# A streaming encoder layer on one core: squares one step earlier, and the first turn of p ahead of the last product

## The chip, the core and the metric

The kernel runs on one core of a Trainium2 chip. The metric is the time of one execution on the device in microseconds (us). TensorE (PE) multiplies, VectorE (DVE), ScalarE (ACT) and GpSimd (POOL) work on tiles, and SyncE (SP), ACT and POOL issue transfers (DMA).

## What is computed

The reference is one layer of an encoder, over a prompt of 2048 frames and over 32 new frames of a running stream, and a last norm. Cut to what matters:

```python
hn = rmsnorm(h, g_mix)
hA, bA, cA, zA, vB, zB = split(hn @ w_in)            # 1024 -> 6 x 512
u = cA * hA;  c = conv3(u) + conv_b;  yA = bA * c * silu(zA)
pooled = trailing_means(vB, windows 2, 4, 8, 16) - vB
yB = (pooled @ pool_w) * pool_scale * silu(zB)
h = h + concat(yA, yB) @ w_out                        # 1024 -> 1024
gate = sigmoid(rmsnorm(h, g_ple) @ w_ple_gate)        # 1024 -> 1024
h = h + (p @ w_ple) * gate                            # the embedding: 256 -> 1024
y = rmsnorm(h, g_final)
```

The last rows of u and v are returned as states.

## The kernel before

All products are made in parts: each f32 operand is split into a high part (a cast, on ACT) and the rest (a subtraction, on DVE; `split`, L77), and a product is the sum of three matmuls of such parts. Most products of four quarters are formed with seven in place of eight, from sums of quarters, so DVE also adds and subtracts quarters of weights and of frames.

**First stage: w_in.** The 2080 frames are five blocks of 416, in three groups: blocks 0 and 1, blocks 2 and 3, block 4 (`GROUPS`, L27; the loop at L1134). Each group runs four units, one for each 128 channels. A unit of the first two groups makes three pairs of products (`Unit.seven`, L899): zb with v (names zbv), c with h (ch), za with b (zab). A pair (L859) has seven products of twelve matmuls into three banks X, Y, Z: X takes quarters 11, S2, S3 and 22, and between them its partial sums are read out. The product S3 can only start when ACT has copied the sum after S2 out (`carry`, L871), and the last product, 22, when DVE has added the sum after S3 into its place (`out`, L874; for zab this is the addition U<-x_zab).

While the second group computes, its spare time on the other engines prepares block 4 (`last_block`, L1059): it is handed to the pairs as `aside`, and for every three steps of the pairs one of its steps is taken (`at_pace`, L1164), from the second unit on. Block 4 has four pieces of rows (128, 128, 128, 32). For a piece c, `scale(c)` takes the squares of its rows with their sum (`x_stat`, L397, and `sumsq`, L87: one activation on ACT over 1024 columns, then two small instructions on POOL for the inverse root, L70 and L74), loads the next piece's rows, and scales the rows in four instructions on DVE (L1098, tile xs) that are kept in program order; POOL stores them (L1100), SP loads them back in blocks (xb, L1106), DVE turns them in place (L1112), and ACT and DVE split them in halves that POOL stores (b_d). In one step of `last_block` the squares, the root and the scaling of a piece come one directly after the other.

**Second stage: W_out.** Pairs of tiles of 128 frames run through `seven` (L211): X, Y, Z again, with calls that hang between the products (`between`). Called with `late`, it makes the products in this order: 11, S2, S1, S3 (all but the S1 add to X, which ends in the last), 12 with 21 (Y), S4 (Z), `step(6)` at L261, and 22 with T4 (X, the last; x_o<-wo_T, 12 matmuls). The loop is at L1288; its last pair is i = 14 (`NT - 3`). The short tile of 32 frames is made ahead of that pair.

**Third stage: the embedding.** `embed` (L105) makes p @ w_ple for the remaining 14 tiles. For a tile, `prep` loads p for four tiles at a time (ep, L122), turns it on PE with two transposes into a bank of its own (ptp, L131; there are two such banks), and splits it (pps, L132 by way of L78 and L79); `run` calls it up to two tiles ahead, makes two halves of six matmuls (e, L103), and ACT copies them out (L148) for a store. Its weight is loaded and split by `embedding_chunks` (wqr, wq, L1310). The embedding's first `prep` runs after the loop of W_out. Beside it ACT and DVE make the quarters of the gate weight (wg) from rows that SP loads (wg_r, L1343).

**Fourth stage: the gate.** Pairs of tiles again (x_g, y_g, z_g), the sum with h by accumulating transfers on POOL (L1396), and the last norm. Rows of h come back in blocks (hn, L1367) and are turned on DVE.

The order of the instructions on each engine is set by the scheduler that builds the program, from the order in which the code is written; instructions under `keep_in_program_order` keep their written order.

Of the kernel before, what the change touches and what calls it, by code (L numbers as in the profile page):

```python
# [9 lines left out]
F32 = mybir.dt.float32  # L10
F32R = mybir.dt.float32r
# [4 lines left out]
P = 128  # L16
D = 1024
# [9 lines left out]
NT = SEQ // P + 1  # L27
NH = D // 2
KH = KC // 2
EARLY = 3  # L30
LATE = 2
# [4 lines left out]
def trunk(ctx, tc, x_p, x_s, c_conv, c_pool, p_p, p_s, g_mix, w_in, conv_w, conv_b, pool_w,  # L36
# [16 lines left out]
    def bank(name):  # L53
        return ps_m.tile([P, 512], F32, tag="mm", name=name)
# [156 lines left out]
    def seven(name, A, W, carry, out, between={}, late=False, in_parts=False, first_tile=False):  # L211

        step = lambda c: between[c]() if c in between else None
        frames_late, weights_late = (FINE, FINE[::2] + FINE[1:2]) if in_parts else (None, None)  # L220
        X, Y, Z = (bank(f"{c}_{name}") for c in "xyz")

        def lower(*parts):
            for ks in parts:
                product(Z, A["S1"], W["T1"], P, ks.start == 0, ks)
            return carry(Z, (1, 1)) if ks.stop == KH else None

        parts = range(KH // 2), range(KH // 2, KH)
        product(X, A["11"], W["11"], P, True, order=frames_late)
        c1 = carry(X, (0, 0))  # L230
        step(1)

        def upper():
            product(Y, A["12"], W["21"], P, True, order=weights_late)
            out(Y, c1, (0, 0))

        if not late:
            upper()
        if in_parts:
            lower(parts[0])  # L240
        step(2)
        product(X, A["S2"], W["T2"], P, False)
        c2 = carry(X, (0, 1))
        step(3)
        c3 = lower(parts[1]) if in_parts else lower(range(KH))
        step(4)

        def right():
            product(Z, A["S4"], W["22"], P, False, order=weights_late)
            out(Z, c2, (0, 1))  # L250

        if first_tile:
            right()
        product(X, A["S3"], W["T3"], P, False)
        out(X, c3, (1, 1))
        step(5)
        if late:
            upper()
        if not first_tile:
            right()  # L260
        step(6)  # L261
        product(X, A["22"], W["T4"], P, False)
        out(X, None, (1, 0))
# [44 lines left out]
    def ring4(t, name):  # L308
        return t.tile([P, D], F32, tag="t", name=name)
# [21 lines left out]
    with ExitStack() as s1:  # L331
# [65 lines left out]
        def x_stat(x, later=False):  # L397

            t, n, name = x
            return t, n, sumsq(t, n, name, later=later)  # L400
# [79 lines left out]
        def staged(name):  # L480
            return xin.tile([P, KH, 2, P], F32R, tag="t", name=name)
# [107 lines left out]
        for c, x in enumerate([*ahead0, short0]):  # L589
            normal(x)  # L590
            n = P if c < 3 else DEC
# [442 lines left out]
        ahead = {}  # L1034

        def load_ahead(g, c):
            ahead[g, c] = columns_in(g, c) if g == 1 else [x_load(f"4_{c}", [x_rows(4, c)])]
# [21 lines left out]
        def last_block():  # L1059

            load_ahead(2, 0)
            back = {}

            def scale(c):
                x = x_stat(ahead.pop((2, c))[0], True)
                if c < 3:
                    load_ahead(2, c + 1)
                scaled_to_memory(x, c * P)
                return x[1]

            def halves_to_memory(c, n):
                u = turned_in_place(back.pop(c))
                for half in range(2):
                    t = staged(f"b_4_{c}_{half}")[:, :, :, :n]
                    v = lambda h: t[:, :, h].rearrange("p k (g t) -> p k g t", t=32)
                    tc.keep_in_program_order(split(v(0), v(1), u[:, half * KH:half * KH + KH]))
                    nc.gpsimd.dma_start(b_d[:, half * KH:half * KH + KH, :, c * P:c * P + n], t.bitcast(F32))
                    yield

            for c in range(5):  # L1080
                n = scale(c) if c < 4 else 0
                yield
                if c:
                    yield from halves_to_memory(c - 1, m)
                if n:
                    back[c], m = from_memory(c * P, n), n
                yield

        xs_d = tc.dram_tile([NB, D], F32, name="xs_d")
# [12 lines left out]
        def from_memory(r, n):  # L1102

            t = ring4(xin, f"xb_{r}")[:, :n * KC]
            for q in range(4):
                nc.sync.dma_start(t[q * 32:q * 32 + 32].rearrange("p (g c) -> p g c", c=256),  # L1106
                                  xs_d[r:r + n, q * 256:q * 256 + 256].rearrange("(g p) c -> p g c", p=32))
            return t
# [24 lines left out]
        for gi, tbs in enumerate(GROUPS):  # L1133
            if gi == 2:  # L1134

                frames_in.close()
                t = slot("hn_4")
# [3 lines left out]
                W = sums_slots("wo")  # L1141
                nc.sync.dma_start(g_bc, g_fin.partition_broadcast(P))
                ya = ctx.enter_context(tc.tile_pool(name="ya", bufs=5, side="right"))
# [31 lines left out]
    with ExitStack() as s2:  # L1175
        pool = lambda name, bufs: s2.enter_context(tc.tile_pool(name=name, bufs=bufs, reuse_waits="tile"))
        w3, qa, xh, st, ss, cmb = (pool(*a) for a in (
            ("w3", 1), ("qa", 1), ("xh", 3), ("st", 4), ("ss", 3), ("cmb", 8)))
# [13 lines left out]
        def h_ops(x, n, name, bare=False, two=False):  # L1192

            add = lambda o, a, b: nc.vector.tensor_tensor(o, a, b, op=ALU.add)

            def carry(ps, at):
                t = st.tile([P, NH], F32, tag="t", name=f"c_{name}_{at[0]}{at[1]}")
                if bare and at != (1, 0):
                    nc.scalar.copy(t[:n], ps[:n])  # L1199
                    return t  # L1200
                add(t[:n], ps[:n], half_of(x, at, n))
                if two:
                    add(t[:n], ps[n:2 * n], t[:n])
                return t

            def out(ps, c, at):
                t = half_of(x, at, n)
                if bare and at != (1, 0):
                    add(t, t, c[:n])
                    c = None  # L1210
                add(t, ps[:n], t if c is None else c[:n])
                if two:
                    add(t, ps[n:2 * n], t)

            return carry, out
# [61 lines left out]
        S = {}  # L1277
# [4 lines left out]
        def next_gate():  # L1282
# [2 lines left out]
                rest_gate()  # L1285
            waiting[:] = [scale_gate(k) for k in [next(gate_rows, None)] if k is not None]

        for i in range(0, NT - 1, 2):  # L1288
            with tc.issue_after(loaded[-1].ins):
                x = [load_rows(xh, "x", i + b, x_p) for b in range(2)] if i else [first_x, second_x]  # L1290
            seven(f"o{i}", S.pop(i), W, *h_ops(x, P, f"o{i}", i == 0), {0: {1: rest}, 2: {3: next_gate}}.get(i, {}), True, i == 0)
            for b in range(2):
                done_h(i + b, x[b])
            last = i + 4 == NT - 1
            if last:
                n = tiles[NT - 1][1]
                A = short("yl", load_y(NT - 1, n), n)
            if i + 2 < NT - 1:

                with tc.issue_after(loaded[-1].ins), tc.issue_after(hold[-1].ins):  # L1300
                    more = prep_h(i + 2)
                more()
            if last:
                x = load_rows(xh, "x", NT - 1, x_p, x_s)
                plain("ol", A, W, n, *h_ops([x], n, "ol", two=True))
                done_h(NT - 1, x)
            next_gate()


        def embedding_chunks(name, rings=(ya, ya)):  # L1310
            wp = []
            for k in range(2):
                raw = ring4(rings[k], f"{name}r_{k}")
                nc.sync.dma_start(raw, w_ple[k * P:(k + 1) * P])
                t = [cmb.tile([P, KH, 2, P], F32R, tag="c", name=f"{name}_{k}_{h}").rearrange("p a b c -> p (a b c)")
                     for h in range(2)]
                split(t[0], t[1], raw)
                wp.append(t)
            return wp

        wp = embedding_chunks("wq")

        rest_e = [*range(EARLY, NT - 2), NT - 1]

        def ring(what, i):
            if what == "pps":
                return st.tile([P, 2, 2, P], F32R, tag="t", name=f"pps_{i}")
            if what == "out" and i not in rest_e[-LATE:]:
                return cmb.tile([P, D], F32, tag="c", name=f"eout_{i}")
            return ring4(ya, f"e{what}_{i}")  # L1330

        _, run = embed(rest_e, wp, ring)
        for c in range(len(rest_e) - LATE):
            run(c)

# [1 line left out]
        W = sums_slots("wg")  # L1337
# [267 lines left out]
        S = {}  # L1605
        n = tiles[NT - 1][1]
# [5 lines left out]
        h, e = (load_rows(*a) for a in ((xh, "h", NT - 1, h_d), (ya, "e", NT - 1, e_d)))  # L1612
# [20 lines left out]
        for i in range(0, NT - 3, 2):  # L1633
            A = S.pop(i)
            steps = prep_g(i + 2)
            e = [load_rows(ya, "e", i + b, e_d) for b in range(2)]
# [32 lines left out]
```

## Time and profile before

| | |
|---|---|
| time, median of 3 runs | 920.71 us (919.93 to 922.12) |
| the profiled execution's own time | 921.88 us |
| its span | 920.1 us |
| PE busy | 906.1 us, 98% of the span |
| weight loads (PEld) busy | 820.7 us, 89% |
| DVE busy | 722.8 us, 79% |
| ACT busy | 477.8 us, 52% |
| POOL busy | 150.9 us, 16% |
| traffic of HBM | 202 GB/s over the span |

Busy shares are averages over stages with different limits. Matmuls are pipelined, so that the time of one (0.35 to 0.4 us) is longer than its distance to the next; what a stall of PE costs is seen from the starts of its instructions. Times in the views count from the start of the span. A tile's name stands without its number, so that one name can be several tiles.

### The profile page before, as it was taken

How to read it: one execution, taken by the hardware profiler on the slowest of the kernel's cores; microseconds unless marked ns; L12 is line 12 of the kernel's file. 1: busy time of each engine (PE TensorE's matmuls, PEld its weight loads, DVE VectorE, ACT ScalarE, POOL GpSimd, SP SyncE). 2: the span in 40 equal slices, each digit the busy share in tenths (PEclk: the TensorE clock that was granted, in tenths of full speed). 3: DMA queues.
4: the chain of work that ended last, by engine and by line, in shares of the span. 5: the costliest groups of instructions: out<-in, count | busy, mean ns of one | idle time of the engine just before them, and what ended most of it. 6: DMA issues, size and time to landing. Idle time of an engine off the chain costs nothing.

```text
span 920.1 us, 12935 instructions
## 1 busy us (share of the span) xinstructions
PE 906.1 (98%) x4485; PEld 820.7 (89%) x4485; DVE 722.8 (79%) x1231; ACT 477.8 (52%) x883; POOL 150.9 (16%) x271
## 2 busy tenths in 40 slices
PE   7999999999999999999999999999999999999996
PEld 5999999999999999999999988888877868888885
DVE  6996999999488989785777688765554798888965
ACT  6744565555335455443545356334334785465555
POOL 3111322212001111000000011111111002233333
PEclk9999999999999999999999999999999999999998
DMA  8345585769935556358655359855774886799893
GB/s 244 98 150 155 150 265 164 212 194 308 420 118 171 186 156 191 99 180 281 195 169 171 127 185 302 273 184 173 246 231 154 298 272 154 185 229 237 213 258 102
DMA packets 140734, 186.37 MB, mean 203 GB/s; under 512 B 12060, under 2 KB 111260, under 8 KB 139389
## 3 DMA queue, kind: packets, MB, share of 16 engines
q1 hardware_dynamic: 120237, 126.33, 45.0%
q0 software_dynamic: 17696, 53.71, 19.9%
q10 hardware_dynamic: 2736, 5.51, 1.8%
q8 instruction: 35, 0.57, 0.2%
q14 instruction: 30, 0.25, 0.1%
HBM read 128.93 MB, written 56.56 MB: 202 GB/s over the span
## 4 chain that ended last, share of the span: by engine, by line
PE 91%; DVE 3%; DMA 2%; issue 2%; ACT 1%; POOL 0%; SPq 0%; DVEq 0%; ACTq 0%; POOLq 0%
PE x_o L168 9%; PE x_zbv L564 7%; PE x_ch L564 7%; PE x_zab L564 7%; PE x_g L168 6%; PE e L103 5%; PE z_o L168 4%; PE z_zbv L564 3%; PE z_ch L564 3%; PE z_g L168 3%; PE z_zab L564 3%; PE v L564 3%; PE c L564 3%; PE b L564 3%; PE za L564 3%; PE h L564 3%
## 5 line engine op out<-in xcount | busy, mean ns | idle before, releaser
L103 PE MATMUL e<-wq,pps 128*128 128x512 f32 (+1 forms) x156 | 38.9, 399 | 0.2 <-ACT pps L78 0.2
L78 ACT CAST y_S<-y_fS 128x512 fp32r<-128x512 f32 x32 | 19.3, 621 | 38.1 <-PE x_o L168 20.1
L168 PE MATMUL x_o<-wo_b,y_S 128*128 128x512 f32 x128 | 35.8, 391 | 0.0
L168 PE MATMUL x_g<-wg_b,g_S 128*128 128x512 f32 x128 | 35.7, 389 | 0.0
L564 PE MATMUL z_zbv<-B,w_zbv_S 128*128 128x416 f32 x168 | 34.2, 352 | 0.0
L564 PE MATMUL x_ch<-B,w_ch_S 128*128 128x416 f32 x168 | 34.1, 351 | 0.0
L564 PE MATMUL z_zab<-B,w_zab_S 128*128 128x416 f32 x168 | 34.1, 351 | 0.0
L564 PE MATMUL x_zab<-B,w_zab_S 128*128 128x416 f32 x168 | 34.0, 351 | 0.0
L564 PE MATMUL x_zbv<-B,w_zbv_S 128*128 128x416 f32 x168 | 34.0, 351 | 0.0
L564 PE MATMUL z_ch<-B,w_ch_S 128*128 128x416 f32 x168 | 34.0, 350 | 0.0
L1396 POOL DMA_DIRECT2D e<-h_d x28 | 24.8, 906 | 53.5 <-DVE e L1393 46.2
L103 PEld LDWEIGHTS e<-wq,pps 128*128 128x128 f32 (+1 forms) x156 | 27.4, 182 | 6.9 <-ACT pps L78 0.5
L564 PEld LDWEIGHTS x_zab<-B,w_zab_S 128*128 128x128 f32 x168 | 31.3, 188 | 0.4
L564 PEld LDWEIGHTS x_zbv<-B,w_zbv_S 128*128 128x128 f32 x168 | 31.4, 188 | 0.3
L564 PEld LDWEIGHTS z_ch<-B,w_ch_S 128*128 128x128 f32 x168 | 31.4, 188 | 0.3
L564 PEld LDWEIGHTS z_zab<-B,w_zab_S 128*128 128x128 f32 x168 | 31.3, 188 | 0.3
L564 PEld LDWEIGHTS x_ch<-B,w_ch_S 128*128 128x128 f32 x168 | 31.3, 188 | 0.3
L564 PEld LDWEIGHTS z_zbv<-B,w_zbv_S 128*128 128x128 f32 x168 | 31.3, 188 | 0.4
L70 POOL TENSOR_SCALAR ms_x<-ssq_x 128x1 f32<-128x1 f32 (+2 forms) x18 | 10.9, 603 | 124.9 <-ACT junk L89 124.8
L78 ACT CAST y<-y 128x512 fp32r<-128x512 f32 x24 | 14.8, 618 | 30.3 <-PE z_o L168 12.9
L168 PEld LDWEIGHTS x_o<-wo_b,y_S 128*128 128x128 f32 x128 | 24.0, 188 | 5.1 <-ACT c_o L1199 0.3
L168 PEld LDWEIGHTS x_g<-wg_b,g_S 128*128 128x128 f32 x128 | 24.0, 188 | 5.0
(592 smaller groups left out, 2650.3 us busy)
## 6 DMA issues: line engine op xcount, KB each, us to landing
y<-y_d SPq DMA_DIRECT2D x16, 512.0 KB, 5.9
x<-in_x_prompt_dram SPq DMA_DIRECT2D x16, 512.0 KB, 5.4
h_d<-x SPq DMA_DIRECT2D x16, 512.0 KB, 2.6
hn<-h_d SPq DMA_DIRECT2D x61, 128.0 KB, 6.7
xt<-in_x_prompt_dram SPq DMA_DIRECT2D x15, 512.0 KB, 6.0
e<-e_d SPq DMA_DIRECT2D x15, 512.0 KB, 5.9
e<-h_d POOLq DMA_DIRECT2D x28, 256.0 KB, 6.6
out_dram<-e POOLq DMA_DIRECT2D x13, 512.0 KB, 4.0
```

Of the source, the lines that this page charges most:

```text
L70: nc.gpsimd.tensor_scalar(ms[:n], ssq[:n], scalar1=1.0 / D, scalar2=EPS, op0=ALU.mult, op1=ALU.add)
L78: ins = nc.scalar.copy(hi, src)
L103: nc.tensor.matmul(ps[:n], pps[:, a, k, :n], wp[k][b][:, cs], start=k + q == 0, stop=k == 1 and q == 2)
L168: nc.tensor.matmul(ps[:n], lhs[:, k, a, :n], w[b][:, k], start=start and k + q == 0, stop=k == KH - 1 and q == 2, skip_group_check=True)
L564: nc.tensor.matmul(ps[:, :NB], lhs[:, k, x], b[:, k, y], start=start and k + q == 0, stop=stop and k == KH - 1 and q == 2, skip_group_chec ...
L1396: nc.gpsimd.dma_start(ee, h_d[r:r + P, at[1] * NH:at[1] * NH + NH], accum_op=ALU.add)
```

## The change

There are two edits. In `last_block`, the squares of a piece and its root are taken out of `scale`: the first piece's are made ahead of the loop, and those of piece c + 1 after piece c's rows are loaded back, one step ahead of the scaling that needs them. In the second and third stage, the list of the embedding's tiles, its ring of buffers and `embed` itself stand ahead of the loop of W_out; the list of weights is empty there and filled after the loop; and the first `prep` (load, two transposes and split for the embedding's first tile) is called as `step(6)` of the last pair, ahead of its last product.

```diff
-            def scale(c):
-                x = x_stat(ahead.pop((2, c))[0], True)
+            def scale(c, x):
                 if c < 3:
                     load_ahead(2, c + 1)
                 scaled_to_memory(x, c * P)
...
+            stat = lambda c: x_stat(ahead.pop((2, c))[0], True)
+            x = stat(0)
             for c in range(5):
-                n = scale(c) if c < 4 else 0
+                n = scale(c, x) if c < 4 else 0
                 yield
                 if c:
                     yield from halves_to_memory(c - 1, m)
                 if n:
                     back[c], m = from_memory(c * P, n), n
+                if c < 3:
+                    x = stat(c + 1)
                 yield
...
+        rest_e = [*range(EARLY, NT - 2), NT - 1]
...
+        wp = []
+        turn_e, run = embed(rest_e, wp, ring)
+
         for i in range(0, NT - 1, 2):
...
-            seven(f"o{i}", S.pop(i), W, *h_ops(x, P, f"o{i}", i == 0), {0: {1: rest}, 2: {3: next_gate}}.get(i, {}), True, i == 0)
+            seven(f"o{i}", S.pop(i), W, *h_ops(x, P, f"o{i}", i == 0), {0: {1: rest}, 2: {3: next_gate}, NT - 3: {6: lambda: turn_e(0)}}.get(i, {}), True, i == 0)
...
-        wp = embedding_chunks("wq")
...
-        _, run = embed(rest_e, wp, ring)
+        wp.extend(embedding_chunks("wq"))
         for c in range(len(rest_e) - LATE):
             run(c)
```

What it does to the order of instructions is shown at three places. The first is the last pair (zab) of the second group's second unit, first on ACT. Before, from the first copy out of x_zab on (junk is the square's output, xt the rows of the third piece, raw_zbv the next unit's weights):

```order
L871 COPY V_1_2808<-x_zab_1_3141 128x416
L78 CAST w_zbv_2_11_3304<-raw_zbv_2a 128x4x128
L78 CAST w_zbv_2_12_3320<-raw_zbv_2a 128x4x128
L931 ACTIVATE V_1_2808<-V_1_2808 128x416
L871 COPY V_1_2808<-x_zab_1_3141 128x416
L78 CAST w_zbv_2_S_3342<-raw_zbv_2a 128x4x128
L871 COPY U_1_2809<-z_zab_1_3143 128x416
L89 ACTIVATE junk,ssq_x_2_3216<-xt_2_2981 128x1024
```

and now, from the same copy on:

```order
L871 COPY V_1_2808<-x_zab_1_3141 128x416
L89 ACTIVATE junk,ssq_x_2_3165<-xt_2_2981 128x1024
L78 CAST w_zbv_2_11_3304<-raw_zbv_2a 128x4x128
L78 CAST w_zbv_2_12_3320<-raw_zbv_2a 128x4x128
L931 ACTIVATE V_1_2808<-V_1_2808 128x416
L871 COPY V_1_2808<-x_zab_1_3141 128x416
L871 COPY U_1_2809<-z_zab_1_3143 128x416
L78 CAST w_zbv_2_S_3342<-raw_zbv_2a 128x4x128
```

The square has moved ahead of seven instructions. On DVE at the same place, before, from the last split of this pair's weights (w_zab) to the addition that the pair's last product waits for:

```order
L79 TENSOR_TENSOR w_zab_1_22_3267<-raw_zab_1b,w_zab_1_22_3267 128x4x128
L539 TENSOR_TENSOR raw_zbv_2b<-raw_zbv_2a,raw_zbv_2b 128x512
L874 TENSOR_TENSOR V_1_2808<-y_zab_1_3142,V_1_2808 128x416
L79 TENSOR_TENSOR w_zbv_2_11_3304<-raw_zbv_2a,w_zbv_2_11_3304 128x4x128
L79 TENSOR_TENSOR w_zbv_2_12_3320<-raw_zbv_2a,w_zbv_2_12_3320 128x4x128
L905 TENSOR_TENSOR c_s_1_2810<-c_s_1_2810,V_1_2808 128x416
L539 TENSOR_TENSOR raw_zbv_2a<-s_zbv_2_3294,raw_zbv_2a 128x512
L539 TENSOR_TENSOR raw_zbv_2a<-raw_zbv_2a 128x512
L79 TENSOR_TENSOR w_zbv_2_S_3342<-raw_zbv_2a,w_zbv_2_S_3342 128x4x128
L1098 SCALAR_TENSOR_TENSOR xs_3224<-xt_2_2981,rstd_x_2_3220,g_bc 128x256 x4
L874 TENSOR_TENSOR U_1_2809<-x_zab_1_3141,U_1_2809 128x416
```

and now, from the instruction behind that split to the same addition:

```order
L1101 SCALAR_TENSOR_TENSOR xs_3224<-xt_2_2981,rstd_x_2_3169,g_bc 128x256 x2
L874 TENSOR_TENSOR V_1_2808<-y_zab_1_3142,V_1_2808 128x416
L1101 SCALAR_TENSOR_TENSOR xs_3224<-xt_2_2981,rstd_x_2_3169,g_bc 128x256 x2
L905 TENSOR_TENSOR c_s_1_2810<-c_s_1_2810,V_1_2808 128x416
L539 TENSOR_TENSOR raw_zbv_2b<-raw_zbv_2a,raw_zbv_2b 128x512
L79 TENSOR_TENSOR w_zbv_2_11_3304<-raw_zbv_2a,w_zbv_2_11_3304 128x4x128
L79 TENSOR_TENSOR w_zbv_2_12_3320<-raw_zbv_2a,w_zbv_2_12_3320 128x4x128
L539 TENSOR_TENSOR raw_zbv_2a<-s_zbv_2_3294,raw_zbv_2a 128x512
L539 TENSOR_TENSOR raw_zbv_2a<-raw_zbv_2a 128x512
L79 TENSOR_TENSOR w_zbv_2_S_3342<-raw_zbv_2a,w_zbv_2_S_3342 128x4x128
L79 TENSOR_TENSOR w_zbv_2_S_3358<-s_zbv_2_3294,w_zbv_2_S_3358 128x4x128
L874 TENSOR_TENSOR U_1_2809<-x_zab_1_3141,U_1_2809 128x416
```

The four scalings have moved from directly ahead of the addition U to the front, in two twos, and one more split of the next weights (S_3358) now stands ahead of U.

The second place is the end of W_out on PE. Before, from the last product but one (z_o) on:

```order
L168 MATMUL z_o_6609<-wo_d_5414,y_S_6540 128x512
L168 MATMUL x_o_6607<-wo_T_4173,y_22_6543 128x512 x12
L131 MATMUL ptp_6735<-ident,ep_6732 128x128 x2
L131 MATMUL ptp_6741<-ident,ep_6732 128x128 x2
L103 MATMUL e_0_6753<-wq_0_6722,pps_6734 128x512
L103 MATMUL e_0_6753<-wq_1_6723,pps_6734 128x512
L103 MATMUL e_1_6761<-wq_0_6722,pps_6734 128x512
L131 MATMUL ptp_6747<-ident,ep_6732 128x128 x2
```

and now:

```order
L168 MATMUL z_o_6609<-wo_d_5414,y_S_6540 128x512
L131 MATMUL ptp_6694<-ident,ep_6691 128x128 x2
L168 MATMUL x_o_6607<-wo_T_4173,y_22_6543 128x512 x12
L131 MATMUL ptp_6741<-ident,ep_6691 128x128 x2
L131 MATMUL ptp_6747<-ident,ep_6691 128x128 x2
L103 MATMUL e_0_6753<-wq_0_6730,pps_6693 128x512
L103 MATMUL e_0_6753<-wq_1_6731,pps_6693 128x512
```

The first turn (ptp) has moved ahead of x_o, and the third ahead of the first product of e; behind these rows the first dozen of e now runs without a turn in it.

The third place is SP in the embedding stage, where the rows of the gate weight are loaded. Before:

```order
L1343 DMA wg_r_1_7024<-g_d 128x1024
L1367 DMA hn_7132<-h_d 32x4x256
L1343 DMA wg_r_0_7045<-g_d 128x1024
L149 DMA e_d<-eout_6752 128x1024
L149 DMA e_d<-eout_6776 128x1024
```

and now:

```order
L1347 DMA wg_r_1_7024<-g_d 128x1024
L1371 DMA hn_7132<-h_d 32x4x256
L149 DMA e_d<-eout_6752 128x1024
L149 DMA e_d<-eout_6776 128x1024
L1347 DMA wg_r_0_7045<-g_d 128x1024
```

The third load of the gate weight's rows stands behind the first two stores of e, which wait for their copies. Further up on the same queue the load of p for the first four tiles has taken the place of the first load of w_ple, and the two loads of w_ple each go one place later.

More of the change, by code (lines that the diff above doesn't have):

```diff
@@ L1286, in next_gate, with ring @@
             waiting[:] = [scale_gate(k) for k in [next(gate_rows, None)] if k is not None]
+        rest_e = [*range(EARLY, NT - 2), NT - 1]
+        def ring(what, i):
+            if what == "pps":
+                return st.tile([P, 2, 2, P], F32R, tag="t", name=f"pps_{i}")
+            if what == "out" and i not in rest_e[-LATE:]:
+                return cmb.tile([P, D], F32, tag="c", name=f"eout_{i}")
+            return ring4(ya, f"e{what}_{i}")
+        wp = []
+        turn_e, run = embed(rest_e, wp, ring)
         for i in range(0, NT - 1, 2):
@@ L1319, in embedding_chunks @@
             return wp
-        wp = embedding_chunks("wq")
[L1323 to L1330, printed above, removed]
-        _, run = embed(rest_e, wp, ring)
+        wp.extend(embedding_chunks("wq"))
         for c in range(len(rest_e) - LATE):
```

## The prediction

> **What bounds the kernel now.** I read first who waits for whom, for PE alone over the whole span. Each row names the waiting group, what released it, the total in us, how often, and the longest single wait.
>
> ```profile
> PE pt L416 <- DVE xt L407: 3.0, 2, 2.3
> PE gm L376 <- DVE V L704: 2.3, 1, 2.3
> PE pt L416 <- PE pt L416: 0.5, 1, 0.5
> PE x_zab L564 <- DVE U L874: 0.3, 1, 0.3
> PE e L103 <- ACT pps L78: 0.2, 1, 0.2
> ```
>
> These are all the waits of PE that the view lists, and they add up to 6.3 us. The first three belong to the start of the kernel. So PE is the bound, and a change that only reorders work can win nothing but such waits. The last two rows are the places that this change touches: the product x_zab of the second group, which waits for an addition on DVE, and the first embedding product, which waits for ACT. The idle times in these rows are too small, because the end of a matmul is modelled (it overlaps the next one); I measure a stall by the starts instead.
>
> **First part: the squares.** The timeline around the first wait (start, duration, engine, line, operation, tiles, count; in brackets the idle time ahead and what ended it):
>
> ```profile
> 319.87 0.69 DVE L539 TENSOR_TENSOR raw_zbv_2a<-raw_zbv_2a 128x512 f32<-128x512 f32 x1
> ...
> 320.58 0.69 DVE L79 TENSOR_TENSOR w_zbv_S<-raw_zbv_2a,w_zbv_S 128x512 fp32r<-128x512 f32 x1
> ...
> 321.20 2.43 PE L564 MATMUL x_zab<-B,w_zab_S 128*128 128x416 f32 x12
> ...
> 321.86 1.06 ACT L89 ACTIVATE junk<-xt 128x1024 bf16<-128x1024 f32 x1
> ...
> 323.10 0.19 POOL L70 TENSOR_SCALAR ms_x<-ssq_x 128x1 f32<-128x1 f32 x1 [16.46 <-ACT junk L89]
> ...
> 323.37 0.56 POOL L74 TENSOR_TENSOR rstd_x<-ms_x,nhalf 128x1 f32<-128x1 f32 x1
> 323.47 2.43 PE L564 MATMUL z_zab<-B,w_zab_S 128*128 128x416 f32 x12
> ...
> 323.97 1.67 DVE L1098 SCALAR_TENSOR_TENSOR xs<-xt,rstd_x,g_bc 128x256 f32<-128x256 f32 x4 [2.69 <-POOL rstd_x L74]
> 325.56 0.58 DVE L874 TENSOR_TENSOR U<-x_zab,U 128x416 f32<-128x416 f32 x1
> ...
> 326.19 2.53 PE L564 MATMUL x_zab<-B_T,w_zab 128*128 128x416 f32 x12 [0.30 <-DVE U L874]
> ```
>
> The reader is to see a queue, not a slow instruction. Twelve products take 323.47 - 321.20 = 2.27 us, so the last product of this pair was due at 323.47 + 2.27 = 325.74. It began at 326.19: **0.45 us lost**. It adds into the bank that the addition U reads, and U stood on DVE behind the four scalings xs, which had waited 2.69 us for the root, which had waited for the square on ACT. The sum x_zab that U needs was done at 321.20 + 2.43 = 323.63.
>
> After the change the square stands directly behind the first copy out of x_zab on ACT, and the scalings stand ahead of the whole preparation of the next weights on DVE. I work the new time of U out from these rows and two more:
>
> ```profile
> 314.60 0.51 ACT L871 COPY V<-x_zab 128x416 f32<-128x416 f32 x1 [1.68 <-PE x_zab L564]
> ...
> 315.00 0.63 ACT L78 CAST w_zbv<-raw_zbv_2a 128x512 fp32r<-128x512 f32 x1
> ...
> 316.16 0.68 DVE L539 TENSOR_TENSOR raw_zbv_2b<-raw_zbv_2a,raw_zbv_2b 128x512 f32<-128x512 f32 x1
> ```
>
> The square takes the place of the cast at 315.00. From its start to that of the scalings lie 323.97 - 321.86 = 2.11 us, so they start at 317.11; DVE is free from 316.16 and idles 0.95 us. The four scalings take 325.56 - 323.97 = 1.59. Then come the same eight instructions that before ran from 316.16 to the end of the split at 321.27 (5.11 us), one more split of weights (0.69), and U (0.58): it ends at 317.11 + 1.59 + 5.11 + 0.69 + 0.58 = 325.08. That is 0.66 us ahead of the 325.74 at which the product is due. **Gain 0.45 us**, all that there is. What is late next is nothing on PE: the addition V (y_zab into V), now behind two scalings, ends near 317.11 + 0.80 + 0.58 = 318.5, and by the copy's 0.51 us for each, its activation on ACT and the copy out of the second sum behind that are done near 319.5, while the product that needs that copy starts at 321.20. The added DVE wait of 0.95 us holds up these same rows, and they are counted.
>
> The other three pieces' squares move as well, where PE does not wait. The place with the least room there is the same addition in the third unit:
>
> ```profile
> 357.20 0.58 DVE L874 TENSOR_TENSOR U<-x_ch,U 128x416 f32<-128x416 f32 x1
> ...
> 358.03 2.43 PE L564 MATMUL x_ch<-B_T,w_ch 128*128 128x416 f32 x12
> ```
>
> It ended at 357.78, 0.25 us ahead of its product. The change takes the fourth piece's scalings (1.6 us) out from ahead of it and puts two splits (1.3 us by the split's row of 0.69) ahead of it, so it comes no later. Cost nothing; if that is wrong by one split, 0.4 us.
>
> **Second part: the first turn.** The timeline of PE from the last two products of W_out into the embedding:
>
> ```profile
> 702.39 2.88 PE L168 MATMUL z_o<-wo_d,y_S 128*128 128x512 f32 x12
> 705.11 2.89 PE L168 MATMUL x_o<-wo_T,y 128*128 128x512 f32 x12
> 707.84 0.60 PE L131 MATMUL ptp<-ident,ep 128*128 128x128 f32 x4
> 708.68 0.96 PE L103 MATMUL e<-wq,pps 128*128 128x512 f32 x3 [0.24 <-ACT pps L78]
> ...
> 711.79 0.38 PE L131 MATMUL ptp<-ident,ep 128*128 128x128 f32 x2
> 711.92 3.02 PE L103 MATMUL e<-wq,pps 128*128 128x512 f32 x12
> ...
> 714.92 3.00 PE L103 MATMUL e<-wq,pps 128*128 128x512 f32 x12
> ...
> 717.89 3.00 PE L103 MATMUL e<-wq,pps 128*128 128x512 f32 x12
> ```
>
> Twelve products of 512 columns take 705.11 - 702.39 = 2.72 us. In the steady state a turn (two transposes) between two dozens costs 717.89 - 714.92 - 2.72 = 0.25. From the start of x_o to that of the second dozen of e lie 711.92 - 705.11 = 6.81 us before; 5.44 of them are two dozens, so four turns and the wait cost 1.37.
>
> After the change the first turn stands ahead of x_o, the second and third together behind it, the fourth behind the first whole dozen of e. The first and the fourth cost 0.25 each. The pair costs 0.35 to 0.47: four transposes ran in 0.60 where two ran in 0.38, so a second turn beside another adds 0.22 to the 0.13 between a turn's start and the next product or to a lone turn's 0.25. That is 0.85 to 0.97 in place of 1.37: 0.40 to 0.52, taken at **0.45 us**. The split of the first turn has the whole of x_o, 2.72 us, for one cast and one subtraction of half the size of those that took 0.63 and 0.68 above. The bounds: if the turn in front of x_o opens a gap as large as the old one, nothing is won; if every turn came at 0.22 and no wait stayed, 1.37 - 0.88 = 0.49 plus what the trace cannot separate, so I bound it at 0.6.
>
> The load of p now goes out on SP in the place of the embedding weight's first load, and each weight load one place later, all of them ahead of the last two tiles of W_out; nothing waits there. Further on, the load of the gate weights moves behind two stores of e on SP:
>
> ```profile
> 712.63 0.38 SPq L1343 DMA_DIRECT2D wg_r<-g_d  x1
> 713.11 2.81 SPq L149 DMA_DIRECT2D e_d<-eout  x2
> ...
> 718.58 0.62 ACT L78 CAST wg_c<-wg_r 128x512 fp32r<-128x512 f32 x1 [0.88 <-DMA wg_r<-g_d]
> ...
> 741.96 0.69 DVE L79 TENSOR_TENSOR wg_c<-wg_r,wg_c 128x512 fp32r<-128x512 f32 x1
> ...
> 748.08 1.08 PE L271 MATMUL x_gl<-wg_c,gl 128*64 128x512 f32 x4
> ```
>
> It is now issued after the second store, 713.11 + 2.81 - 712.63 = 3.3 us later, and its data come near 721.9 in place of 718.6. The last piece of this quarter of the weights is ready at 742.65 and first needed at 748.08: 5.4 us of cover, 4.5 when PE comes 0.9 us earlier. Cost nothing.
>
> Whether the gain lasts to the end is read from the chain that ended last, which leaves PE in the gate stage:
>
> ```profile
> 767.39 2.73 PE x_g L168 x12
> ...
> 779.74 8.37 DMA e<-h_d
> ...
> 803.32 6.57 DMA hn<-h_d
> ...
> 819.21 3.02 PE x_g L168 x12
> ```
>
> It runs through two transfers, but it starts from a product of PE and comes back to one, so it moves as a whole with PE. The gain stays.
>
> **The sum.** 0.45 + 0.45 = 0.90 us off the profiled execution's own 921.88 (span 920.1 and 1.8 around it): 920.98. That execution lies 1.17 above the median of the three runs, 920.71, so against the median I expect **919.8 us**.
>
> **The rivals.** (a) *Only one part pays*: 920.3. Its mechanism for the first part is a slow root. The two POOL instructions of the root took 0.19 and 0.56 us above, with DVE idle, but for the piece before:
>
> ```profile
> 296.99 1.02 POOL L70 TENSOR_SCALAR ms_x<-ssq_x 128x1 f32<-128x1 f32 x1 [6.95 <-ACT junk L89]
> ...
> 298.10 0.88 POOL L74 TENSOR_TENSOR rstd_x<-ms_x,nhalf 128x1 f32<-128x1 f32 x1
> ```
>
> with DVE busy beside it, 1.15 us more. U would end at 326.23 and nothing would be won there. Against it: DVE has nothing else to run while it waits for the new root. The Trainium skill, SBUF — State Buffer, "Who interferes with whom", says that a DVE instruction with two SBUF inputs and a GpSimd instruction that reads SBUF lock each other out for a whole instruction; by that rule these rows are such a lock, and the earlier root risks it only against the split that ends at 316.24.
>
> (b) *Slower*: the gate weights' chain. If the 3.3 us at its head grow to twice that on the way through ACT's and DVE's queues, the product at 748.08 would wait 6.6 - 4.5 = 2.1 us: 919.8 + 2.1 = 921.9. It decides from 4.5 us on. Against it: the loads behind it on SP move ahead of stores of e, and ACT waited for the data there only 0.88.
>
> (c) *More than the sum*: in front of the product at 819.21 stands a wait of 0.22 us; with the upper bound of the turn both together give 0.45 + 0.6 + 0.22, near 919.4.
>
> (d) *The change does nothing measurable*: the turn opens a new gap and the root is slow: 920.7.
>
> **How the numbers follow.** Forecast 0.60, (a) 0.18, (b) 0.08, (c) 0.07, (d) 0.07. About 0.2% (1.84 us) is what a measurement of this kernel can tell from no change. All cases but the worst of (b) lie inside it; the shown runs alone spread over 2.2 us, so a median can still fall beyond: faster 0.15, the same 0.77, slower 0.08. The range takes (c) less 1 us of that spread and most of (b): 918.4 to 921.6.
>
> **What would show it.** Right: PE waits neither for U nor for pps any more, the third piece's scalings stand near 317, x_zab follows z_zab by 2.27 us, e follows the turns behind x_o without a wait, and the second dozen of e starts 6.4 us after x_o. Wrong: a row in which PE waits for U or V in the second group, POOL rows near 1 us beside the new root, or a wait of x_gl for wg.

## The result and the profile after

The changed kernel takes **924.51 us** (median of 6 runs, 923.6 to 926.24), the kernel before on the same chip 920.34 (6 runs, 919.86 to 922.12): a ratio of 1.0044, 95% interval 1.0032 to 1.0056. It is slower by 4.2 us where 0.9 less was forecast, and above the range of 918.4 to 921.6. The profiled execution took 924.62 us, with a span of 922.8.

The waits of PE after the change, the three largest (waiting group, what released it, total, how often, longest):

```profile
PE x_zbv L564 <- DVE V L874: 2.9, 1, 2.9
PE gm L376 <- DVE V L704: 2.3, 1, 2.3
PE pt L416 <- DVE xt L407: 2.3, 1, 2.3
```

The two waits that the change aimed at, x_zab for U and e for pps, are gone from the view. In their place stands a new one at the top: the last product of x_zbv, in the third unit of the second group, waits 2.9 us for the addition V on DVE.

**The first place did what was forecast.** Timeline of the changed kernel (start, duration, engine, line, operation, tiles; idle time ahead in brackets). On ACT the square stands six instructions earlier, directly behind the first copy out of x_zab. This execution is 1.93 us ahead of the one before already at z_zab (321.54 against 323.47), for reasons at its start (1.94 us already at 100 us, x_ch at 101.69 for 103.63):

```profile
313.07 1.06 ACT L89 ACTIVATE junk<-xt 128x1024 bf16<-128x1024 f32 x1
...
314.59 0.56 POOL L74 TENSOR_TENSOR rstd_x<-ms_x,nhalf 128x1 f32<-128x1 f32 x1
315.18 0.88 DVE L1101 SCALAR_TENSOR_TENSOR xs<-xt,rstd_x,g_bc 128x256 f32<-128x256 f32 x2 [0.87 <-POOL rstd_x L74]
...
321.54 2.43 PE L564 MATMUL z_zab<-B,w_zab_S 128*128 128x416 f32 x12
322.16 0.58 DVE L874 TENSOR_TENSOR U<-x_zab,U 128x416 f32<-128x416 f32 x1
...
323.81 2.43 PE L564 MATMUL x_zab<-B_T,w_zab 128*128 128x416 f32 x12
```

x_zab follows z_zab by 323.81 - 321.54 = 2.27 us, the time of one dozen: the stall of 0.45 us is gone. Another 0.1 us goes with it: a dozen that begins behind a wait takes 2.53 us (x_zab at 326.19 before), one without 2.43. The scalings start 2.11 us behind the square, as before.

**The loss stands 15 us later**, at the fourth piece of rows, the one with 32 rows. Its place in the kernel before (g_bc, xt, xs: scaling of the fourth piece; b_d: the store of split rows by POOL):

```profile
333.32 0.90 POOL L1077 DMA_DIRECT2D b_d<-b  x1 [6.77 <-DVE b L79]
...
340.28 0.58 DVE L874 TENSOR_TENSOR V<-x_zbv,V 128x416 f32<-128x416 f32 x1
...
342.16 2.43 PE L564 MATMUL x_zbv<-B_T,w_zbv 128*128 128x416 f32 x12
...
346.70 2.43 PE L564 MATMUL y_ch<-B,w_ch 128*128 128x416 f32 x12
...
347.98 0.47 DVE L1098 SCALAR_TENSOR_TENSOR xs<-xt,rstd_x,g_bc 32x256 f32<-32x256 f32 x1 [0.72 <-POOL rstd_x L74]
```

and after the change:

```profile
330.21 0.96 POOL L1076 DMA_DIRECT2D b_d<-b  x1 [5.25 <-DVE b L79]
...
333.31 0.68 DVE L79 TENSOR_TENSOR b<-xb,b 128x512 fp32r<-128x512 f32 x1
337.41 2.43 PE L564 MATMUL z_zbv<-B,w_zbv_S 128*128 128x416 f32 x12
338.62 1.66 DVE L1101 SCALAR_TENSOR_TENSOR xs<-xt,rstd_x,g_bc 32x256 f32<-32x256 f32 x4 [4.63 <-issue]
...
342.13 0.58 DVE L874 TENSOR_TENSOR V<-x_zbv,V 128x416 f32<-128x416 f32 x1
...
342.77 4.53 PE L564 MATMUL x_zbv<-B_T,w_zbv 128*128 128x416 f32 x12 [2.93 <-DVE V L874]
...
347.09 3.17 PE L564 MATMUL x_ch<-B,w_ch 128*128 128x416 f32 x12
350.11 2.43 PE L564 MATMUL y_ch<-B,w_ch 128*128 128x416 f32 x12
```

Before, the scalings ran at 347.98, behind V. Now they stand ahead of V, directly behind a split that ended at 333.99, and DVE stood still in front of them for 4.63 us. "issue" says that the view knows no releaser; the order of the built program names the semaphores that the instruction waits for. DVE's row now and, below it, the row before:

```
L1101 SCALAR_TENSOR_TENSOR xs_3453<-xt_3_3222,rstd_x_3_3399,g_bc 32x256 [waits DMAHW6_49,DMASW4_49,Pool_49]
L1098 SCALAR_TENSOR_TENSOR xs_3453<-xt_3_3222,rstd_x_3_3451,g_bc 32x256 [waits Pool_49]
```

DMAHW6 is the load of the rows, which the square had read long before; DMASW4 is the store b_d that POOL issued at 330.21. The tile xs comes from a ring of five buffers. Before, it got the buffer of xb, which ACT and DVE had read themselves; allocated earlier, it gets the buffer of the first half of b of the second piece, and must wait until the store that reads that half has landed. The time to landing of this one store, issued at 330.21:

```profile
DMA to landing us min/median/max: 8.3/8.3/8.3
```

330.21 + 8.3 = 338.5, and the scalings began at 338.62. The squares alone, a run of its own below, repeat it: the store is issued at 332.05, lands after 8.3 us too, at 340.35, and DVE goes on 0.1 us later:

```profile
340.46 1.66 DVE L1101 SCALAR_TENSOR_TENSOR xs<-xt,rstd_x,g_bc 32x256 f32<-32x256 f32 x4 [4.63 <-issue]
```

Behind the scalings on DVE stood two splits, a sum of weights and then V: the last product of x_zbv was due at 337.41 + 2.27 = 339.68 and began at 342.77, **3.09 us lost**.

**And PE came back at half its clock.** Windows of 1 us (busy time and count of PE, PEld, DVE, ACT, POOL; then the granted clock, the share of the DMA engines, GB/s):

```profile
341.00:342.00 1.00, 0.00 (x0) 0.00 (x0) 0.96 (x2) 0.00 (x0) 0.12 (x1) 0.95 0.74 188
342.00:343.00 1.00, 0.23 (x1) 0.23 (x2) 1.00 (x3) 0.00 (x0) 0.00 (x0) 0.50 0.86 266
...
347.00:348.00 1.00, 1.00 (x4) 0.95 (x4) 0.13 (x1) 0.67 (x2) 0.00 (x0) 0.50 0.33 97
348.00:349.00 1.00, 1.00 (x5) 0.97 (x5) 1.00 (x2) 0.36 (x1) 0.00 (x0) 0.64 1.09 330
349.00:350.00 1.00, 1.00 (x7) 0.99 (x6) 1.00 (x2) 0.00 (x0) 0.00 (x0) 1.00 0.33 97
```

The clock was 0.50 from 341.9 (0.95 over that window is 0.1 us of half clock) to 348.7: 6.8 us. The two dozens from 342.77 to 350.11 took 7.34 us where 2 x 2.27 = 4.54 is their time: **2.80 us lost** again.

**The second place did what was forecast**, too:

```profile
705.81 2.88 PE L168 MATMUL z_o<-wo_d,y_S 128*128 128x512 f32 x12
708.53 0.38 PE L131 MATMUL ptp<-ident,ep 128*128 128x128 f32 x2
708.67 3.01 PE L168 MATMUL x_o<-wo_T,y 128*128 128x512 f32 x12
711.52 0.60 PE L131 MATMUL ptp<-ident,ep 128*128 128x128 f32 x4
711.87 3.02 PE L103 MATMUL e<-wq,pps 128*128 128x512 f32 x12
...
714.86 3.00 PE L103 MATMUL e<-wq,pps 128*128 128x512 f32 x12
```

From z_o to the second dozen of e lie 714.86 - 705.81 = 9.05 us; before it was 711.92 - 702.39 = 9.53. The turn gained 0.48, and the dozens run without a wait between them.

The whole account, as the start of the same instruction after less before:

| instruction | after - before | the step |
|---|---|---|
| z_zab, second group, second unit | -1.93 | the start of the kernel, ahead of the change |
| its last x_zab | -2.38 | -0.45, first part |
| z_zbv, next unit | -2.49 | -0.11, the shorter dozen of x_zab |
| its last x_zbv | +0.61 | **+3.10**, the wait for V |
| y_ch | +3.41 | **+2.80**, the half clock |
| z_o, end of W_out | +3.42 | +0.01 |
| second dozen of e | +2.94 | -0.48, second part |
| x_g on wg_T, first of the gate | +3.14 | +0.20 |
| end of the span | +2.7 | -0.4, small waits of x_g in the gate stage that are not there now |

The steps of the change add up to -0.56 + 5.90 - 0.48 = +4.9 us; the medians say +4.2, with an interval of 2.9 to 5.2.

### The profile page after: what moved, and what is told of

Its sections match the earlier page's. It is cut to its first block, busy times and chain, and to the rows that moved or that the text cites. A ratio compares the mean times of both kernels' runs of the same rounds, so it can differ in the third digit from the quotient of the medians.

```text
span 922.8 us, 12940 instructions
## 1 busy us (share of the span) xinstructions
PE 906.4 (98%) x4485; PEld 821.0 (89%) x4485; DVE 722.9 (78%) x1231; ACT 477.8 (52%) x883; POOL 149.8 (16%) x271
## 4 chain that ended last, share of the span: by engine, by line
PE 92%; DVE 3%; issue 2%; ACT 1%; POOL 1%; DMA 1%; DVEq 0%; POOLq 0%; ACTq 0%
PE x_o L168 9%; PE x_g L168 9%; PE x_ch L564 7%; PE x_zbv L564 6%; PE x_zab L564 6%; PE e L103 5%; PE z_g L168 5%; PE z_o L168 4%; PE z_ch L564 3%; PE c L564 3%; PE z_zbv L564 3%; PE b L564 3%; PE za L564 3%; PE h L564 3%; PE z_zab L564 3%; PE zb L564 2%
## 5 line engine op out<-in xcount | busy, mean ns | idle before, releaser
L1197 DVE TENSOR_TENSOR c_o<-x_o,x 128x512 f32<-128x512 f32 x14 | 9.7, 689 | 23.9 <-PE x_o L168 23.9
```

## The experiments

**Theory (slot)**: the loss is the wait of the fourth piece's scalings for a store that still reads their buffer, with the half clock behind it. **Rivals**: the second edit takes part in it (turn); the early place of these scalings in DVE's queue costs by itself (place). Four kernels ran on one chip, beside 32 runs of the kernel before (921.53 us). The times expected below were worked out from 920.3 us, the kernel before on the chip of the result, so they are compared as ratios: 919.4 us stands for 0.9990, 919.8 for 0.9995, 921 for 1.0007, 925.0 for 1.0051.

**One part alone.** The turn alone (`last_block` as before) and the squares alone (W_out as before):

> Only the second part of the change: the first turn of p ahead of x_o; the squares stand where they stood before. Theory (slot): the whole loss lies in the fourth piece's scalings, which wait on DVE for the store that still reads their buffer; the turn itself gains the 0.48 us seen between z_o and the second dozen of e. Then 920.3 - 0.5 = 919.8 us, and PE has no wait for V. Rival (turn): the turn, or the loads that it moves on SP, takes part in the loss; then over 921 us.

> Only the first part: all three squares a step ahead; W_out's end as before. Theory (slot): the loss is whole here and the turn's 0.48 us is missing: 924.5 + 0.5 = 925.0 us, with the wait of x_zbv for V of 2.9 us and about 7 us of half clock on PE behind it. Rival (turn): part of the loss belongs to the other edit; then clearly below 924.5 us.

The squares alone: 925.02 us, ratio 1.0036 (1.0024 to 1.0048); the turn alone: 922.06, ratio 1.0004 (0.9995 to 1.0013). The squares alone lose within noise what the whole change loses (1.0044), and the turn alone at most 1.0013, so the loss belongs to the squares. That 925.02 meets the expected 925.0 is luck of the chip: as a ratio, 1.0036 misses 1.0051, and of the 7 us of half clock that were expected its profile has 3.4. These two do not exclude that a small part of it belongs to the turn, since the rival's 1.0007 lies in the interval of the turn alone; the next two kernels have the turn and not the loss, and with them the rival (turn) falls. The squares' profile has the same wait:

```profile
PE x_zbv L564 <- DVE V L874: 2.9, 1, 2.9
```

The turn alone came out 0.0009 above its 0.9995, which is the lower end of its interval. Between z_o and the second dozen of e it did gain 0.49 (702.84 to 711.88 in its profile, 9.04 for 9.53), but PE had lost 1 us in W_out's first pair, at a wait that DVE handed on (y_fS needs rows of y that SP loads):

```profile
563.82 0.69 DVE L194 TENSOR_TENSOR y_fS<-y,y 128x512 f32<-128x512 f32 x1 [1.24 <-DMA y<-y_d]
```

In the kernel before, the same instruction waited 0.26. All engines have the same instructions up to there in both kernels, so it ran once more, on another chip:

> The kernel with the turn alone, once more: its first time was 1.0004 of the kernel before (0.9995 to 1.0013), where 0.9995 was expected, and its profile showed one wait that no other has, x_o for c_o, 0.52 us, behind a load of y at W_out's start, in front of all that the turn changes. Theory (such a wait comes and goes with the load, whichever kernel runs): a ratio of 0.9995 within the interval, the gain of 0.48 us between z_o and the second dozen of e, and the wait for c_o smaller or gone. Rival (the turn costs as much elsewhere as it gains): 1.000 or more again, and the same wait.

921.22 us, ratio 0.9991 (0.9981 to 1.0002): 0.9995 lies in the interval, and the rival's 1.000 as well. The wait was there again (1.22 us). In the other twelve profiles it was between nothing and 0.73, so whether it belongs to this kernel or comes and goes is open. The turn stands 140 us later, and the seven profiles with 0.20 us or less there are all of kernels that have it, so the turn by itself does not bring the wait.

**The fourth piece left where it was.**

```diff
             for c in range(5):
+                if c == 3:
+                    x = stat(c)
                 n = scale(c, x) if c < 4 else 0
...
-                if c < 3:
+                if c < 2:
                     x = stat(c + 1)
```

> Both parts, but the square of the fourth piece (32 rows) stays in its old step; the second and third pieces' go ahead. Theory (slot) and rival (place: the early place of the fourth piece's scalings in DVE's queue costs by itself) agree here: no wait of PE for V, for U or for pps, 920.3 - 0.45 - 0.48 = 919.4 us. If the time stays above 921 us, both are wrong and something else in the change loses the time.

920.22 us, ratio 0.9986 (0.9977 to 0.9995), with the expected 0.9990 inside. PE has none of the three waits, and x_zbv follows z_zbv by 340.56 - 338.29 = 2.27:

```profile
338.29 2.43 PE L564 MATMUL z_zbv<-B,w_zbv_S 128*128 128x416 f32 x12
340.56 2.43 PE L564 MATMUL x_zbv<-B_T,w_zbv 128*128 128x416 f32 x12
...
346.37 0.47 DVE L1103 SCALAR_TENSOR_TENSOR xs<-xt,rstd_x,g_bc 32x256 f32<-32x256 f32 x1 [0.71 <-POOL rstd_x L74]
```

In this kernel, too, xs has the buffer of that half of b and the same wait for its store in the program; but it stands at 346.37, behind V, and by then the store, issued at 331.11, has landed (8.1 us, at 339.2). So the buffer alone does not cost anything. Whether the early place alone does, the next one tells.

**The early place kept, the buffer not.** Rows 32 to 63 of the tile that brings the fourth piece are unused; the scaled rows go there:

```diff
-            t = ring4(xin, f"xs_{r}")
+            t = ring4(xin, f"xs_{r}") if n == P else xt[n:]
```

> The whole change, but the fourth piece's scaled rows are written into the unused rows 32 to 63 of the tile that its own rows came in, so they need no slot of the ring of five and wait for no store. Their place in DVE's queue is as early as in the change, or earlier. Theory (slot): no wait of x_zbv for V; 919.4 us. Rival (place): the 1.7 us of scalings ahead of the additions U and V still hold PE up; 921 us or more, with a wait of PE for U or V in the second group.

**920.00 us, ratio 0.9982 (0.9973 to 0.9990)**, the lowest of the four, level with the last one within the intervals, and better than both kernels. The expected 0.9990 is the upper end of its interval. In the program the scalings keep the wait for the load of their rows (DMAHW6) and lose the one for the store (DMASW4), which excludes the load as the cause. DVE runs the four scalings between 327.12 and 333.44, ahead of V and without a wait, and V is still in time:

```profile
327.12 0.47 DVE L1101 SCALAR_TENSOR_TENSOR xt<-xt,rstd_x,g_bc 32x256 f32<-32x256 f32 x1
...
339.50 0.58 DVE L874 TENSOR_TENSOR V<-x_zbv,V 128x416 f32<-128x416 f32 x1
...
341.11 2.43 PE L564 MATMUL x_zbv<-B_T,w_zbv 128*128 128x416 f32 x12
```

x_zbv follows z_zbv (338.85) by 2.26 us, without a wait. So neither the early place nor the buffer costs by itself; both together do, and rival (place) falls. One version more has the squares this way and no turn:

> The squares ahead and the fourth piece's scaled rows in the unused rows of its own tile, W_out's end as it was before the change. Theory (slot): the first part alone then wins the 0.45 us at x_zab and loses nothing at x_zbv: before less 0.45, a ratio near 0.9995; against the kernel with the turn as well (ratio 0.9982, interval 0.9973 to 0.9990) it lacks 0.48 us, 0.0005. Rival (the turn is worth nothing in the end, since a later wait gives it back): the same ratio as with the turn, 0.9982. One more question: the gaps between the last products of W_out and the gate stage, x_o on wo_T to x_g on wg_T, were 67.56 before and 67.98 in the run without the turn, 67.24 to 67.39 in the four runs with it, counted from the turn's transposes; here the theory wants 67.6 or more.

921.04 us against 921.24 on its chip, ratio 0.9992 (0.9984 to 1.0001). Theory asked for 0.9995, and for a gain 0.0005 smaller than with the turn; it is 0.0010 smaller, with intervals as wide as that. The rival's 0.9982 lies just outside. The gap from x_o to x_g was 67.96 us here (67.56 before, 67.98 with the squares alone) and 67.10 to 67.26 in the profiles with the turn, 67.24 to 67.39 from its transposes on. The three profiles without the turn differ by 0.4 among themselves, so this shows that a later wait does not take all of the turn's 0.48 us, and not how much of it stays: 0.2 to 0.3 against the kernel before, 0.6 to 0.7 against the other two.

**How much of the loss is the clock.** To set the idle time of PE by hand, further readers of x_zbv's bank were put behind the addition V in the version with own rows; they leave V as it is:

```diff
                 half_product(X, make("S3"), B["T3"], False)
                 out(X, (1, 1))
+                for _ in range(N if name == "zbv_1_2" else 0):
+                    nc.vector.scalar_tensor_tensor(D[1, 1], X[:, :NB], 0.0, D[1, 1], op0=ALU.mult, op1=ALU.add)
```

> The version with the fourth piece in its own rows, and on DVE two further instructions behind the addition V of x_zbv, each V = 0 * x_zbv + V: they read the bank that x_zbv's last product adds into, so that product waits for them. From the rows of the version without them the last is done 1.2 us after the product was due. Theory (the half clock behind the stall comes from the length of the idle time, from about 2 us on, as the granted clock fell 2.1 us after PE's last product ended): 1.2 us lost and no more, the clock stays 1.00, 920.0 + 1.2 = 921.2 us on the same chip as that version. Rival (any wait of PE for DVE here costs as much again in clock): 2.4 us.

> As the run before, with three such instructions: about 2.2 us idle by the rows. Theory (length, from about 2 us on): at the edge, the clock falls late or not at all; 2.2 us lost, 2.8 more if it falls. Rival (any wait costs as much again): 4.4 us.

> As before, with four such instructions and one transposition between them that waits for its rows: about 4.1 us idle by the rows. Theory (length): the granted clock is 0.50 for some 7 us, as in the changed kernel, so 4.1 us of idle time and about 2.8 us of slow products: 920.0 + 6.9 = 926.9 us. Rival (the clock loss grows with the idle time, as much again): 8.2 us, 928.2 us. Rival (the half clock in the changed kernel had another cause than the idle time): 924.1 us and no clock below 1.00.

All three missed: 920.00, 919.89 and 920.64 us, ratios 0.9988, 0.9987 and 0.9988, as if nothing had been added. PE's rows in the last one tell why:

```profile
339.82 2.43 PE L564 MATMUL x_ch<-B,w_ch 128*128 128x416 f32 x12
342.08 1.87 PE L564 MATMUL y_ch<-B,w_ch 128*128 128x416 f32 x9
344.23 2.53 PE L564 MATMUL x_zbv<-B_T,w_zbv 128*128 128x416 f32 x12 [0.28 <-DVE V L892]
```

The scheduler had put 21 matmuls of the next pair ahead of the late product (six and twelve in the other two). So the same kernels were made once more with PE's products of these two pairs pinned to their written order (`keep_in_program_order` on each matmul):

> As the run with two further readers of x_zbv's bank, but PE's products of these two units are held in the order that they have without the readers, so that no other product can go ahead. By that run's rows the last reader is done 1.1 us after the product was due. Theory (the half clock depends on the length of the idle time, from about 2 us on): 1.1 us idle, clock 1.00 throughout, 920.0 + 1.1 = 921.1 us. Rival (as much again in clock): 922.2 us.

> The same with three readers: about 2.1 us idle. Theory (length): on the edge; 922.1 us if the clock stays, 924.9 us if it falls. Rival (as much again): 924.2 us.

> The same with four readers and a transposition between them that waits for its rows: about 4.3 us idle. Theory (length): half clock for about 7 us, 2.8 us more: 920.0 + 7.1 = 927.1 us. Rival (as much again): 928.6 us. Rival (the half clock of the changed kernel had another cause): 924.3 us, no clock below 1.00.

Times: 921.32 us (ratio 0.9996, 0.9987 to 1.0005), 923.68 (1.0015, 1.0002 to 1.0027) and 927.12 (1.0052, 1.0035 to 1.0069, from four runs). As ratios the theory asked for 0.9995, 1.0006 (1.0037 if the clock falls) and 1.0060: the first and the last lie in their intervals, and of the middle pair the lower. The rivals' 1.0007, 1.0029 and 1.0077, and 1.0030 for another cause, lie outside. The last product of x_zbv in the three, in this order:

```profile
342.71 2.54 PE L564 MATMUL x_zbv<-B_T,w_zbv 128*128 128x416 f32 x12 [1.06 <-DVE V L895]
```

```profile
342.21 2.53 PE L564 MATMUL x_zbv<-B_T,w_zbv 128*128 128x416 f32 x12 [2.06 <-DVE V L895]
```

```profile
344.48 4.53 PE L564 MATMUL x_zbv<-B_T,w_zbv 128*128 128x416 f32 x12 [4.26 <-DVE V L895]
```

With 1.06 and 2.06 us idle the dozen takes 2.53 to 2.54 us, as x_zab behind its wait before the change, and the clock stays 1.00 in every window; with 4.26 it takes 4.53, as in the changed kernel. Together with the two kernels that have the loss (lost idle time: start of x_zbv less z_zbv's start less 2.27; by clock: start of y_ch less that of x_zbv less 4.54; the 0.1 us of the first two rows is the longer dozen behind a wait and no loss of clock):

| kernel | idle by the view | lost idle | half clock lasted | lost by clock |
|---|---|---|---|---|
| two pinned | 1.06 | 1.21 | - | 0.1 |
| three pinned | 2.06 | 2.21 | - | 0.1 |
| the change | 2.93 | 3.09 | 6.8 | 2.8 |
| squares alone | 2.94 | 3.10 | 3.4 | 1.6 |
| four pinned | 4.26 | 4.42 | 6.8 | 2.3 |

The theory of length holds in these five profiles, one of each kernel: no loss of clock up to 2.06 us, one from 2.93 on, and it does not grow with the idle time. "As much again" is refuted by the first two rows, "another cause" by the last. Over the version with own rows (0.9982) the medians lie 1.3, 3.0 and 6.4 us, where the profiles have 1.3, 2.3 and 6.7. The first and the last agree. In the middle one the ten runs spread: four, the profiled one among them, took 921.75 to 922.18 us, the other six 923.62 to 925.6 (the kernel before on that chip: 920.08 to 924.78). Whether the clock fell in those six at 2 us of idle time no profile shows, so the length at which it begins to fall is open between 1.06 and 2.93 us.

## Why the prediction was wrong, point by point

- **PE is the bound, and a reordering can win only its waits**: right. What the prediction left out is the other direction: a reordering can make a new wait, and it checked one place for that.
- **First part, the third piece's square**: right, in place and size. Scalings forecast at 317.11, found at 315.18 in an execution 1.93 ahead; gain 0.45 forecast, 0.45 found, and 0.11 more in the dozen behind the wait, which the sum did not have. The root took 0.19 and 0.56 us, so rival (a) did not come.
- **"The other three pieces' squares move as well, where PE does not wait. ... Cost nothing"**: this is **the step that failed**. It followed the fourth piece's scalings out of the place that they left (the third pair's U<-x_ch, with 0.25 us of room) and not into the place that they went to, 12 us up DVE's queue (from 347.98 to behind the split that ended at 335.94 before), ahead of V<-x_zbv, which had 342.16 - 340.86 = 1.30 us of room; and it did not ask what they wait for there. Their buffer had become that of a tile which a store by POOL still read. Measured: 4.63 us of standstill on DVE, 3.09 us on PE, 2.80 us more by the clock, against "if that is wrong by one split, 0.4 us".
- Could it have been priced from the profile before? In part. The product that waits for V would start about 4.2 us behind the scalings: by the rows before, 1.6 us of scalings, 2.0 for the two splits and the sum behind them, 0.58 for V. After the change it is 342.77 - 338.62 = 4.15, and this is used here. The stores of b_d from 320 to 380 us landed, before the change, after

```profile
DMA to landing us min/median/max: 4.5/5.7/6.2
```

  so from the store at 333.32 on PE would go on at 333.32 + 4.5 to 6.2 + 4.15 = 341.97 to 343.67, for a product due at 342.16: a loss of nothing to 1.5 us. That the store took 8.3 us, and that PE's clock would fall, no row of before showed. At its upper end, 1.5 us, such a rival would have outweighed the gain of 0.9 and had a quarter of the 5.9 us; at its lower end it would have cost nothing.
- **Second part, the turn**: right; 0.45 forecast (0.40 to 0.52), 0.48 and 0.49 found. The second dozen of e starts 714.86 - 708.67 = 6.19 us behind x_o, against 6.4 forecast: the first turn, which now lies ahead of x_o, belongs to the sum, and with it the distance is 6.33.
- **The gate weights' load, rival (b)**: the load in question went out at 718.88 for 712.63, 3.3 us later beside a PE that was 2.94 later; no product waited for it, x_gl began at 750.99 for 748.08. Cost nothing, as forecast.
- **"The gain stays"**: right for the chain; 0.20 us and -0.4 us of waits on the way to the end are of the size that one profile differs from the next. The wait of 0.22 in front of the product at 819.21, which rival (c) named, is not there after the change; but other kernels with the first part and the turn still lose 0.3 to 0.4 us at that place (a pair of tiles takes 19.47 us in the kernel with two squares ahead, 19.32 in "two pinned", 19.39 before and 19.04 after), so it comes and goes.
- **The slower rival**: the sign of being wrong that came is one that the prediction names, a row in which PE waits for V in the second group, but no rival stood behind it. A slower one was looked for at the gate weights, where nothing was tight. That SP's queue was worked through and DVE's only at one of four places was a choice, and the wrong one.

## What to carry to other kernels

When an edit moves an instruction up an in-order queue, follow it to where it arrives: list its waits there, above all a tile from a ring of buffers, since an earlier allocation can give it a buffer that a store is still reading; then look at what stands behind it. A scheduler fills a wait that it sees coming (21 matmuls went ahead of the late product here) and did not fill this one. A stall of 1.2 us on PE cost 1.3 us here, one of 2.2 us cost 2.3 in its profile and 3.0 by the median, one of 3.1 us cost 4.7 to 5.9: the length at which the clock goes is worth knowing before a stall is priced.

## What the runs showed of the hardware

The granted clock fell to 0.50 at 2.1 us (the change), 2.9 us (squares alone) and 2.3 us (four pinned) after PE's last product had ended, and did not fall in the one profile with 2.06 us of idle time. It stayed there 6.8, 3.4 and 6.8 us, the larger part of it with PE busy. For the squares alone these are the windows at its two ends:

```profile
344.00:345.00 1.00, 0.40 (x1) 0.40 (x2) 1.00 (x3) 0.00 (x0) 0.00 (x0) 0.78 0.95 307
...
347.00:348.00 1.00, 1.00 (x5) 0.95 (x4) 1.00 (x2) 0.00 (x0) 0.00 (x0) 0.52 0.00 0
```

0.78 is 0.44 us of half clock, 0.52 is 0.96, and with the two windows between them that makes 3.4 us. The Trainium skill, TensorE: Matmul & The Clock Gate, "Part 1: The HAM clock gate", describes this gate: half rate after about one idle window of 3.4 us, full rate after one busy window, on windows that run freely. The durations agree with one and two such windows. The length of idle time does not: 2.93 us, less than a window, was enough here twice. The free-running window would explain why two kernels with the same idle time lost 2.8 and 1.6 us; no run here shows its phase. The runs of the squares alone spread from 922.95 to 928.45 us, where those of the kernel before spread over 2.9.
